# A double first group, w in two halves of columns, and tiles that hold every fourth column

## The chip, the cores and the metric

The kernel runs on one core of a Trainium2 chip. The metric is the time of one execution on the device in microseconds (us). "Fast" is the undisturbed state. A time is about 2 us longer than the span that the profile of the same execution shows; times are compared with times, spans with spans. TensorE is written PE in the profile (PEld is its weight load), VectorE is DVE, ScalarE is ACT, GpSimd is POOL, SyncE is SP.

## The reference

```python
B, S, D = (16, 2048, 1024)          # x: [B, S, D], w: [D, D], decay: [D], all float32
xw = x @ w
out[:, 0, :] = xw[:, 0, :]
for t in range(1, S):
    out[:, t, :] = decay[None, :] * out[:, t - 1, :] + xw[:, t, :]
```

A matrix product, then along time a running sum that decays with its own factor in each of the 1024 columns.

## The kernel before

Time is cut into 64 chunks of 512 steps. Chunks go in double groups of 1024 steps, but the first two and the last two chunks are groups of their own. A "tile" is 128 columns of the product for one group, with the columns on the partitions and time along the row, along which the kernel scans. A chunk of x is loaded as bf16 (GpSimd issues it), turned in blocks of 32x32 by VectorE (`turn`), and copied into order by VectorE or ScalarE (`part`). Eight matmuls for each chunk and tile make the product. In three of four tiles ScalarE and GpSimd first fold pairs of steps (`pair`), VectorE scans half the elements, and the other half is filled in (`complete`); every fourth tile is scanned whole by VectorE straight from PSUM. Then VectorE turns the result back into row order (`back`), and it is stored.

The parts that the change touches:

```python
    def matmul(ps, n, k, xt, t0=0, t1=TL):          # n: tile, k: step of the contraction
        pin(nc.tensor.matmul(
            out=ps[:, t0:t1],
            lhsT=wsb[:, k, n].rearrange("p q i -> p (q i)"),      # 128 columns, packed
            rhs=xt[:, k // 2, k % 2, t0:t1],
            start=(k == 0), stop=(k == K - 1)))
    # ... (cut)
        def back(self):
            T, n = self.T, self.n
            pin(nc.vector.transpose(
                out=self.ot[:, :, n * P:(n + 1) * P],             # 32 floats in a row, packed
                in_=self.so[:, 2:T + 2].rearrange("p (i t) -> p i t", t=P)))
            if n == 3:
                self.store(0, 4)
            elif n == 5 and self.final:
                self.store(4, 6)
            elif n == 7:
                self.store(6 if self.final else 4, 8)

        def store(self, n0, n1):
            for q in (0, 2, 1, 3):
                queue = nc.scalar if self.final and q >= 2 else nc.sync
    # ... (cut): the DMA of quarter q
    # head: w comes as whole rows in bf16, and eight copies bring it into the order that wsb has
    for k in range(K):
        copy = nc.scalar.copy if k % 4 == 3 else nc.vector.tensor_copy
        pin(copy(out=wsb[:, k].rearrange("p n q i -> p q n i"), in_=wk[:, k]))
    # ... (cut)
    # single-chunk groups: two tiles share one PSUM tile
                    if n % 2 == 0:
                        both = ring(psp, "ps", 3, [128, 2, TL])
                    ps = both[:, n % 2]
```

Of the kernel before, what the change touches and what calls it, by code (L numbers as in the profile page):

```python
# [9 lines left out]
FP32 = mybir.dt.float32  # L10
BF16 = mybir.dt.bfloat16
ALU = mybir.AluOpType


def _ap(ap_obj: bass.AP, new_ap, extra_offset=0):
    return dataclasses.replace(
        ap_obj,
        ap=[list(p) for p in new_ap],
        offset=ap_obj.offset + extra_offset,
    )  # L20
# [5 lines left out]
def kernel(  # L26
# [21 lines left out]



    nc = tc.nc
    pin = tc.keep_in_program_order
    B, S, D = x.shape
    assert w.shape == (D, D)

    NQ = 4
    P = 32
    CQ = D // NQ
    K = CQ // P
# [1 line left out]
    TL = 512  # L61
    NJ = TL // P
    NC = S // TL
    HEADS = 7

    const = ctx.enter_context(tc.tile_pool(name="const", bufs=1))
    sb = ctx.enter_context(tc.tile_pool(name="sb", bufs=1))
# [8 lines left out]
    def quad(q):  # L76
        return slice(q * P, (q + 1) * P)

    chunks = [(b, c * TL) for b in range(B) for c in range(NC)]
    nch = len(chunks)  # L80
    groups = ([[0], [1]] + [[c, c + 1] for c in range(2, nch - 2, 2)]
              + [[nch - 2], [nch - 1]])
    for g in groups:
        assert chunks[g[0]][0] == chunks[g[-1]][0]

    dec = const.tile([128, K], FP32, name="dec")
    dec2 = psp.tile([128, 512], FP32, name="dec2")
    spare = psp.tile([128, TL], FP32, name="spare")
    wsb = const.tile([128, K, K, NQ, P], BF16, name="wsb")

    def ot_tile():
        return ring(sb, "ot", 2, [128, 2 * NJ, CQ])
# [29 lines left out]
    def matmul(ps, n, k, xt, t0=0, t1=TL):  # L122
        pin(nc.tensor.matmul(  # L123
            out=ps[:, t0:t1],
            lhsT=wsb[:, k, n].rearrange("p q i -> p (q i)"),
            rhs=xt[:, k // 2, k % 2, t0:t1],
            start=(k == 0),
            stop=(k == K - 1),
        ))
# [3 lines left out]
    class Tile:  # L133
# [42 lines left out]
        def scan(self):  # L176
            T, n, so = self.T, self.n, self.so
            if self.paired:
                pin(nc.vector.tensor_tensor_scan(  # L179
                    out=so[:, 3:T + 2:2],  # L180
                    data0=dec2[:, n:n + 1].to_broadcast([128, T // 2]),
                    data1=self.xs[:, 1:T:2],
                    initial=0.0 if self.prev is None else self.prev,
                    op0=ALU.mult,
                    op1=ALU.add,
                ))
            else:
                pin(nc.vector.tensor_tensor_scan(  # L188
                    out=so[:, 2:T + 2],
                    data0=dec[:, n:n + 1].to_broadcast([128, T]),  # L190
                    data1=self.ps,
                    initial=0.0 if self.prev is None else self.prev,
                    op0=ALU.mult,
                    op1=ALU.add,
                ))

        def complete(self):
            T, so = self.T, self.so
# [7 lines left out]
        def back(self):  # L206
            T, n = self.T, self.n
            pin(nc.vector.transpose(  # L208
                out=self.ot[:, :, n * P:(n + 1) * P],
                in_=self.so[:, 2:T + 2].rearrange("p (i t) -> p i t", t=P)))  # L210
            if n == 3:
                self.store(0, 4)
            elif n == 5 and self.final:
                self.store(4, 6)
            elif n == 7:
                self.store(6 if self.final else 4, 8)

        def store(self, n0, n1):
            for q in (0, 2, 1, 3):
                queue = nc.scalar if self.final and q >= 2 else nc.sync  # L220
                pin(queue.dma_start(
                    out=_ap(out, [[D, P], [P * D, self.T // P], [1, (n1 - n0) * P]],
                            (self.b * S + self.t0) * D + q * CQ + n0 * P),
                    in_=self.ot[quad(q), :, n0 * P:n1 * P]))


    with nc.allow_non_contiguous_dma(reason="a vector of 1024"):
        for q in range(NQ):
            nc.sync.dma_start(
                out=dec[quad(q), :], in_=_ap(decay, [[1, P], [P, K]], q * CQ))  # L230
    idle = const.tile([128, TL], BF16, name="idle")
    pin(nc.vector.memset(idle, 0.0))  # L232
    for _ in range(40):
        pin(nc.tensor.matmul(out=spare, lhsT=idle[:, 0:128], rhs=idle, start=True, stop=True))  # L234
    H = NJ // 2
    for j0 in (0, H):
        for q in range(NQ):
            load(0, q, j0, j0 + H)
    wb = ot_tile().rearrange("p j c -> p (j c)")[:, 0:M * D].bitcast(BF16)
    wm = wb.rearrange("p (m d) -> p m d", m=M)  # L240
    for m in range(M):
        for q in range(NQ):
            pin(nc.gpsimd.dma_start(  # L243
                out=wm[quad(q), m],
                in_=_ap(w, [[2 * D, P], [1, 2 * D]], (q * CQ + m * 2 * P) * D)))
    for j0 in (0, H):
        for q in range(NQ):
            load(1, q, j0, j0 + H)
    for q in range(NQ):
        load(2, q)  # L250
    for j0 in (0, H):
        turn(0, j0, j0 + H)
        part(0, nc.vector.tensor_copy, 0, 2, j0, j0 + H)
        part(0, nc.scalar.copy, 2, M, j0, j0 + H)
    pin(nc.vector.tensor_tensor(out=dec2[:, 0:K], in0=dec, in1=dec, op=ALU.mult))
    wk = wb.rearrange("p (k q n i) -> p k q n i", k=K, q=NQ, n=K)
    for k in range(K):
        copy = nc.scalar.copy if k % 4 == 3 else nc.vector.tensor_copy
        pin(copy(out=wsb[:, k].rearrange("p n q i -> p q n i"), in_=wk[:, k]))  # L259


    agenda = {}
# [2 lines left out]
    def at(step, f, *args):  # L265
        agenda.setdefault(step, []).append(lambda: f(*args))

    def turn_and_load(c):
        turn(c)
        if c + 3 < nch:  # L270
            loads.extend((c + 3, q) for q in range(NQ))

    def turn_last_half(c):
        turn(c, H, NJ)
        loads.extend((c + 3, q) for q in range(NQ))

    at(1, turn, 1, 0, H)
    at(1, part, 1, nc.vector.tensor_copy, 0, 2, 0, H)
    at(1, part, 1, nc.scalar.copy, 2, M, 0, H)
    at(3, turn_last_half, 1)  # L280
    at(3, part, 1, nc.vector.tensor_copy, 0, 2, H, NJ)
    at(3, part, 1, nc.scalar.copy, 2, M, H, NJ)
    for gi, g in enumerate(groups):
        for l, c in enumerate(g):
            if c > 1:
                first = gi * K
                ahead = (7, 6, 4) if l or len(g) == 1 else (11, 10, 8)
                at(first - ahead[0], turn_and_load, c)
                at(first - ahead[1], part, c, nc.scalar.copy, 0, 2)
                at(first - ahead[2], part, c, nc.scalar.copy, 2, M)  # L290

    waiting = []

# [16 lines left out]
            if tl is not None and tl.paired == lag:  # L310
                tl.back()

    loads.extend((3, q) for q in range(NQ))
    for gi, g in enumerate(groups):
        T = TL * len(g)
        if len(g) == 2:
            ot = ot_tile()
        else:
            if g[0] in (0, nch - 2):
                halves = ot_tile()  # L320
            ot = halves[:, g[0] % 2 * NJ:(g[0] % 2 + 1) * NJ]
        heads = []
        if gi == 0:
            bank = [ring(psp, "ps", 3, [128, 2, TL]) for _ in range(3)]
            heads = [bank[n // 2][:, n % 2] for n in range(6)] + [spare]
            for k in range(K):
                for n in range(HEADS):
                    matmul(heads[n], n, k, xt_of[0])
        elif gi == 1:
            bank = [ring(psp, "ps", 3, [128, 2, TL]) for _ in range(2)]  # L330
            heads = [bank[n // 2][:, n % 2] for n in range(4)]
            for t0 in (0, H * P):
                for n in range(4):
                    for k in range(K):
                        matmul(heads[n], n, k, xt_of[1], t0, t0 + H * P)
        for n in range(K):
            if n < len(heads):
                ps = heads[n]
            else:
                if len(g) == 2:  # L340
                    ps = ring(psp, "ps", 3, [128, T])
                elif gi == 0:
                    ps = ring(psp, "ps", 3, [128, 2, TL])[:, 0]
                else:
                    if n % 2 == 0:
                        both = ring(psp, "ps", 3, [128, 2, TL])
                    ps = both[:, n % 2]
                for k in range(K):
                    for l, c in enumerate(g):
                        matmul(ps[:, l * TL:(l + 1) * TL], n, k, xt_of[c])  # L350
            behind(Tile(gi, n, ps, ot))
            for f in agenda.pop(gi * K + n, []):
                f()
            for _ in range(2 if len(loads) > NQ else 1):
                if loads:
                    load(*loads.pop(0))
    behind(None)
    behind(None)


# [1 line left out]
_INS = ['x', 'w', 'decay']  # L362
_OUTS = [((16, 2048, 1024), 'float32')]
# [25 lines left out]
```

## Time and profile before

| what | before |
|---|---|
| time, median of 3 runs | 953.86 us (953.14 to 954.48) |
| matmuls | 4096 of 512 columns' worth, 0.2155 us each in the middle |
| TensorE busy, VectorE busy | 95%, 87% of the span |
| first 144 matmuls done | 69.6 us |
| from there to the start of the last two chunks | 825.3 us |
| from there to the end of the last back-transpose | 42.0 us |
| from there to the end of the span | 16.6 us |

The last four rows cut the span of 953.6 us at marks that I count out of the matmul rows of the trace: the moment at which 144 matmuls are done, and the moment at which 3968 are (all but the 128 of the last two chunks). The lines of the profile that show the bound stand in the prediction.

### The profile page before, as it was taken

What the parts mean: (1) busy time and instruction counts of PE and PEld (TensorE: products, weight loads), DVE (VectorE), ACT (ScalarE), POOL (GpSimd) and SP (SyncE); (2) the same over time, 40 slices, a digit from 0 to 9 for tenths busy, and PEclk for the clock granted to TensorE, in tenths of its full rate; (3) what the DMA queues carried; (4) which work ended last, traced back from release to release, by engine and by line L of the source; (5) the groups of instructions that cost most, each with busy time, mean ns of one, the idle gap of its engine ahead of it and who ended that gap; (6) DMA issues with size and microseconds to landing.
All of it is one profiled execution on the core that took longest, in us unless ns stands there. A gap on an engine that the chain in (4) does not pass through costs nothing. (4 is left out here: it accounts for less than half of the span.)

```text
span 953.6 us, 12026 instructions
## 1 busy us (share of the span) xinstructions
PE 904.8 (95%) x4168; PEld 410.6 (43%) x4168; DVE 830.6 (87%) x622; ACT 684.9 (72%) x961; POOL 663.1 (70%) x768
## 2 busy tenths in 40 slices
PE   8669999999999999999999999999999999999871
PEld 3334444444444444444444444444444444444330
DVE  2678999999999999999999999999999999998872
ACT  2468777877777787778777777877787787776550
POOL 8557777777776777777677777767776776765430
PEclk9789999999999999999999999999999999999997
DMA  9999999999999999999999999999999999996628
GB/s 161 170 218 172 223 234 232 225 224 235 224 227 228 237 227 223 233 227 229 226 235 225 228 228 229 231 221 233 224 236 225 229 229 224 234 229 148 145 49 188
DMA packets 405821, 204.23 MB, mean 214 GB/s; under 512 B 14080, under 2 KB 405248, under 8 KB 405760
## 3 DMA queue, kind: packets, MB, share of 16 engines
q1 hardware_dynamic: 266528, 133.19, 57.5%
q0 software_dynamic: 136064, 69.22, 54.0%
q10 hardware_dynamic: 3168, 1.05, 0.6%
q8 instruction: 32, 0.52, 0.2%
q14 instruction: 29, 0.24, 0.1%
HBM read 138.42 MB, written 134.22 MB: 286 GB/s over the span
## 5 line engine op out<-in xcount | busy, mean ns | idle before, releaser
L123 PE MATMUL ps<-xt,wsb 128*128 128x512 bf16 (+1 forms) x4120 | 893.8, 380 | 28.4 <-ACT h L157 16.7
L123 PEld LDWEIGHTS <-wsb 128*128 128x128 bf16 x4128 | 406.4, 98 | 516.6 <-issue 36.0
L173 POOL TENSOR_TENSOR xs<-h,xs 128x512 f32<-128x512 f32 (+1 forms) x195 | 244.7, 1255 | 212.3 <-ACT h L157 92.6
L167 ACT COPY xs<-ps 128x1024 f32<-128x1024 f32 (+1 forms) x194 | 190.4, 982 | 186.1 <-PE ps L123 183.1
L208 DVE STREAM_TRANSPOSE ot<-so 128x1024 f32<-128x1024 f32 (+1 forms) x272 | 303.5, 1154 | 2.2 <-POOL so L201 1.3
L201 POOL TENSOR_TENSOR so<-h,xs 128x512 f32<-128x512 f32 (+1 forms) x195 | 243.6, 1249 | 44.7 <-ACT keep L204 22.4
L120 ACT COPY xt<-xw 128x2048 bf16<-128x2048 bf16 (+1 forms) x128 | 240.1, 1876 | 17.6 <-DVE xw L112 17.6
L102 POOL DMA_DIRECT2D xb<-in_x_dram x264 | 174.8, 663 | 7.9 <-DVE xw L112 6.0
L157 ACT ACTIVATE h<-so,dec 128x512 f32<-128x512 f32 (+1 forms) x195 | 147.3, 755 | 33.4 <-DVE so L179 29.7
L179 DVE TENSOR_TENSOR_SCAN so<-dec,keep,xs 128x512 f32<-128x512 f32 (+1 forms) x101 | 123.6, 1224 | 42.8 <-POOL xs L173 42.5
L112 DVE STREAM_TRANSPOSE xw<-xb 128x2048 f32<-128x2048 f32 (+1 forms) x66 | 146.6, 2221 | 8.1 <-DMA xb<-in_x_dram 8.1
L179 DVE TENSOR_TENSOR_SCAN so<-dec,xs 128x512 f32<-128x512 f32 (+1 forms) x94 | 113.0, 1202 | 41.5 <-POOL xs L173 38.1
L157 ACT ACTIVATE h<-ps,dec 128x512 f32<-128x512 f32 (+1 forms) x194 | 131.5, 678 | 0.0
L188 DVE TENSOR_TENSOR_SCAN so<-dec,keep,ps 128x1024 f32<-128x1024 f32 (+1 forms) x43 | 86.2, 2004 | 4.8 <-PE ps L123 4.6
L188 DVE TENSOR_TENSOR_SCAN so<-dec,ps 128x1024 f32<-128x1024 f32 (+1 forms) x34 | 72.6, 2135 | 0.0
L204 ACT COPY keep<-so 128x1 f32<-128x1 f32 x144 | 26.9, 187 | 0.2 <-DVE so L188 0.2
L172 ACT COPY so<-keep 128x1 f32<-128x1 f32 x101 | 19.3, 191 | 0.0
L234 PE MATMUL spare<-idle 128*128 128x512 bf16 x40 | 10.3, 424 | 1.2 <-DVE idle L232 1.2
L170 POOL MEMSET so<- 128x1 f32 x94 | 11.0, 117 | 0.0
L243 POOL DMA_DIRECT2D ot<-in_w_dram x16 | 8.4, 529 | 2.4 <-DMA xb<-in_x_dram 1.2
L259 DVE COPY wsb<-ot 128x1024 bf16<-128x1024 bf16 x6 | 2.4, 424 | 6.1 <-DMA ot<-in_w_dram 6.1
L234 PEld LDWEIGHTS <-idle 128*128 128x128 bf16 x40 | 4.2, 108 | 6.8 <-issue 1.9
(12 smaller groups left out, 11.3 us busy)
## 6 DMA issues: line engine op xcount, KB each, us to landing
out_dram<-ot SPq DMA_DIRECT2D x240, 512.0 KB, 9.0
xb<-in_x_dram POOLq DMA_DIRECT2D x248, 256.0 KB, 7.5
out_dram<-ot SPq DMA_DIRECT2D x26, 256.0 KB, 6.5
xb<-in_x_dram POOLq DMA_DIRECT2D x16, 128.0 KB, 5.1
ot<-in_w_dram POOLq DMA_DIRECT2D x16, 128.0 KB, 4.8
out_dram<-ot ACTq DMA_DIRECT2D x2, 256.0 KB, 3.5
out_dram<-ot ACTq DMA_DIRECT2D x4, 128.0 KB, 4.0
out_dram<-ot SPq DMA_DIRECT2D x4, 128.0 KB, 3.5
```

What stands on the lines that cost most here:

```text
L102: pin(nc.gpsimd.dma_start(out=xb_of[c][quad(q), j0:j1], in_=_ap(x, [[D, P], [P * D, j1 - j0], [1, CQ]], (b * S + t0 + j0 * P) * D + q * CQ)))
L112: pin(nc.vector.transpose(out=dst.rearrange("p (m j i) -> p j m i", m=M, i=P)[:, j0:j1], in_=src.rearrange("p (j m c) -> p j m c", m=M, c=P)))
L120: pin(copy(out=xt_of[c][:, m0:m1, :, j0 * P:j1 * P], in_=src))
L123: pin(nc.tensor.matmul(out=ps[:, t0:t1], lhsT=wsb[:, k, n].rearrange("p q i -> p (q i)"), rhs=xt[:, k // 2, k % 2, t0:t1], start=(k == 0), ...
L157: pin(nc.scalar.activation(out=h, in_=src, func=mybir.ActivationFunctionType.Copy, scale=dec[:, self.n:self.n + 1]))
L167: pin(nc.scalar.copy(out=self.xs, in_=self.ps))
L173: pin(nc.gpsimd.tensor_tensor(out=self.xs[:, 1:T:2], in0=g, in1=self.xs[:, 1:T:2], op=ALU.add))
L179: pin(nc.vector.tensor_tensor_scan(out=so[:, 3:T + 2:2], data0=dec2[:, n:n + 1].to_broadcast([128, T // 2]), data1=self.xs[:, 1:T:2], init ...
L188: pin(nc.vector.tensor_tensor_scan(out=so[:, 2:T + 2], data0=dec[:, n:n + 1].to_broadcast([128, T]), data1=self.ps, initial=0.0 if self.pr ...
L201: pin(nc.gpsimd.tensor_tensor(out=so[:, 2:T + 2:2], in0=h, in1=self.xs[:, 0:T:2], op=ALU.add))
L204: pin(nc.scalar.copy(out=self.keep, in_=so[:, T + 1:T + 2]))
L208: pin(nc.vector.transpose(out=self.ot[:, :, n * P:(n + 1) * P], in_=self.so[:, 2:T + 2].rearrange("p (i t) -> p i t", t=P)))
```

## The change

Its intent is to shorten both ends. Chunks 0 and 1 become a double group. w comes in two halves of columns, so that matmuls can start on the lower half. The copies that reorder w go: w stays as it is in memory, a tile takes every fourth column of a half, and the price is a stride of four in the weight load and in what the back-transpose writes. At the end each tile gets its own PSUM tile, chunk 63 is turned earlier, and all stores go on one queue.

```diff
-    groups = ([[0], [1]] + [[c, c + 1] for c in range(2, nch - 2, 2)]
-              + [[nch - 2], [nch - 1]])
+    groups = [[c, c + 1] for c in range(0, nch - 2, 2)] + [[nch - 2], [nch - 1]]
-    wsb = const.tile([128, K, K, NQ, P], BF16, name="wsb")
+    wsb = const.tile([128, K, D], BF16, name="wsb")
-            lhsT=wsb[:, k, n].rearrange("p q i -> p (q i)"),
+            lhsT=wsb[:, k, n // R * CH + n % R:(n // R + 1) * CH:R],     # R = 4, CH = 512
...
-                out=self.ot[:, :, n * P:(n + 1) * P],
+                out=self.ot[:, :, n // R * CR + n % R:(n // R + 1) * CR:R],     # CR = 128
-            if n == 3: ...
+            if n % R == R - 1:
+                self.store(n // R)
...
-                queue = nc.scalar if self.final and q >= 2 else nc.sync
+                pin(nc.sync.dma_start(
...
+    def lower(m):      # SyncE, fp32 to a stage; cast(m): DVE and ACT write it to wsb[:, k, 0:CH]
+    def upper(m):
+        for q in range(NQ):
+            pin(nc.gpsimd.dma_start(
+                out=wsb[quad(q), 2 * m:2 * m + 2, CH:D],
+                in_=_ap(w, [[2 * D, P], [D, 2], [1, CH]], (q * CQ + m * 2 * P) * D + CH)))
...
-    for q in range(NQ):
-        load(2, q)
...
+    steps = {2: (3, 3, 4), 3: (4, 5, 6), 4: (7, 8, 10), nch - 1: (-11, -10, -8)}
...
-    loads.extend((3, q) for q in range(NQ))
+    loads.extend((c, q) for c in (2, 3, 4) for q in range(NQ))
...
-                        both = ring(psp, "ps", 3, [128, 2, TL])
-                    ps = both[:, n % 2]
+                if len(g) == 2 or n % 4 < 3:
                     ps = ring(psp, "ps", 3, [128, T])
+                else:
+                    ps = ring(psp, "spare", 1, [128, TL])
```

Cut: the order of the first loads, the order of the first matmuls, and the scan of a tile that lies in two PSUM tiles.

## The prediction

Cut from it, where marked, is what it said of the hardware that no run or trace of this case shows: most of one paragraph, one ground for rival 1 and half a sentence of rival 3. The sum came to 926.5 us, taken as 925. Three of its figures need their source, and all three are in the trace of the kernel before. The 1.04 ns an element of a transpose is (2285 - 1217) / 1024, from the mean times for 2048 and 1024 elements. These 1068 ns for 1024 more elements are also the 1067 of rival 1; that the new step would cost as much again ("at half rate") was my assumption. The 2 ns of a scan is (2260 - 1192) / 512, from whole-row scans of 1024 and 512 elements. Half clock is the granted clock of 0.50 from 14.5 to 17.9 us, where matmuls of 512 columns start 0.43 us apart.

> **What bounds the kernel now.** I read the page first, then the busy time of each engine in stretches, then the waits of TensorE, the start and end in order of time, and last the waits of SyncE's queue.
>
> ```profile
> PE 904.8 (95%) x4168; PEld 410.6 (43%) x4168; DVE 830.6 (87%) x622; ACT 684.9 (72%) x961; POOL 663.1 (70%) x768
> ...
> PEclk9789999999999999999999999999999999999997
> ```
> ```profile
> 100.00:300.00 200.00, 200.00 (x928) 90.68 (x927) 184.99 (x131) 156.22 (x214) 148.78 (x169) 1.00 1.19 228
> ```
> The last line has busy us of PE, PEld, DVE, ACT and POOL, each with its count, then clock, DMA share and GB/s. From 100 to 880 us every such stretch is full of matmuls: 200 us by 928 is 0.2155 us each. The middle is TensorE's; DVE is next with 92.5%, so about 15 us of every 200 are free. The work is 64 chunks by 8 column tiles by 8 steps of k = 4096 matmuls; by 0.2155 that is 882.7 us. So 953.6 - 882.7 = 71 us lie at the two ends, and only they can be won.
>
> ```profile
> PE ps L123 <- ACT h L157: 16.7, 9, 6.6
> PE ps L123 <- DVE so L188: 9.0, 4, 2.9
> PE ps L123 <- DVE wsb L259: 2.7, 1, 2.7
> ```
> ```profile
> 14.20 2.50 PE L123 MATMUL ps<-xt,wsb 128*128 128x512 bf16 x6 [2.71 <-DVE wsb L259]
> ...
> 57.37 6.02 PE L123 MATMUL ps<-xt,wsb 128*128 128x512 bf16 x16 [6.59 <-ACT h L157]
> ...
> 64.44 10.74 PE L123 MATMUL ps<-xt,wsb 128*128 128x512 bf16 x49 [1.05 <-ACT h L157]
> ```
> The head: the first useful matmul is at 14.20, and TensorE is continuous only from 64.44. By my count of the rows 120 matmuls are done by then (25.9 us of work in 50.2 us): idle 15.3 us before it, and half clock around 14.5 to 17.9, 31.6 to 45.2 and 55.4 to 62.3 in the clock record. The single-chunk groups 0 and 1 pay a start-up of the chain copy, add, scan for only 8 matmuls a tile.
>
> ```profile
> 908.94 3.61 PE L123 MATMUL ps<-xt,wsb 128*128 128x512 bf16 x16 [1.58 <-ACT h L157]
> ...
> 927.44 0.92 ACTq L221 DMA_DIRECT2D out_dram<-ot  x2
> ...
> 935.70 1.28 DVE L208 STREAM_TRANSPOSE ot<-so 128x512 f32<-128x512 f32 x2
> ```
> ```profile
> SPq L221 <- DMA out_dram<-ot: 31.6, 4, 25.8
> ```
> ```profile
> 910.00:920.00 10.00, 7.90 (x37) 3.42 (x36) 7.28 (x10) 4.40 (x14) 2.94 (x4) 1.00 0.02 6
> ```
> The tail has two faults. Each pair of tiles shares one two-bank PSUM tile, and the second half waits until ACT has read the first: one wait per 16 matmuls, 10.4 us in all from 897.90. And SyncE's stores stand still for 25.8 us: the DMA share is 0.02 from 910 to 920 although chunk 62 has finished halves. The semaphore that its first store waits for is the one of a store that ACT's queue issued at 927.44 and that landed at 930.44. Eighteen stores then go out after 930; the last back-transpose ends at 936.98, the span at 953.6: 16.6 us of draining.
>
> [...] The trace has only packed loads, 98 ns each. [...] Four bf16 are 8 bytes[...]. But the new back-transpose writes fp32 with a step of four, 16 bytes[...]. No instruction of this trace writes so, and this is the largest open point.
>
> **The change, part by part.**
> (a) Head. Chunks 0 and 1 become a double group; w comes in two column halves, the lower by SyncE as fp32 and cast on chip, the upper cast in the DMA straight to its place. Tiles 0 to 3 need only the lower half, and with the stride a tile holds every fourth column of a half; the loads of the upper half queue behind chunk 1. The copies that reordered w on chip go (eight, 0.42 us on DVE and 1.04 on ACT); eight casts of 512 columns take their place, inside the wait for chunk 0. In the issue rows of the head, transfers of 256 KB read landed 0.63 to 0.70 us apart, about 0.4 MB per us. The last load of chunk 0 landed at 11.07. The first quarter of lower w adds 0.5 MB (1.2 us, part of it in an idle queue), and the rest shares the engines with the end of chunk 0, say 1.5 us: landing near 13.5. Transpose 1.25 and copy 0.69 give a first matmul near 15.5, 1.3 later than now. Thirty-two matmuls, eight at half clock (0.43 each, as at 14.2 now): 24.1. Chunk 1 is in by then (6.3 MB at 0.416 from about 4.5 is 19.6; with its transpose and copy 22). Thirty-two half matmuls of 0.11 to 27.6, 16 full ones to 31.0. Tile 4 ends at 34.4, tile 5 at 37.9. Now the chain behind TensorE must keep up, with these durations of one instruction (busy us in all, then mean ns, after the bar):
>
> ```profile
> L208 DVE STREAM_TRANSPOSE ot<-so 128x1024 f32<-128x1024 f32 x240 | 282.9, 1217 | 0.8
> L120 ACT COPY xt<-xw 128x2048 bf16<-128x2048 bf16 x124 | 235.9, 1903 | 5.0 <-DVE xw L112 5.0
> L173 POOL TENSOR_TENSOR xs<-h,xs 128x512 f32<-128x512 f32 x180 | 233.6, 1298 | 198.6 <-ACT h L157 89.3 <-ACT so L172 58.0 <-issue 45.8
> L167 ACT COPY xs<-ps 128x1024 f32<-128x1024 f32 x180 | 182.3, 1013 | 171.9 <-PE ps L123 168.9 <-POOL so L201 1.4 <-issue 0.2
> L157 ACT ACTIVATE h<-ps,dec 128x512 f32<-128x512 f32 x180 | 124.8, 693 | 0.0
> ```
> Tile 0 is complete at 26.7; copy 1.01 and scale 0.69 bring it to 28.4, POOL's add 1.30 to 29.7. Chunk 2 is loaded only behind that add, because POOL works in program order: two issues of 0.66 to 31.0, tile 1's add to 32.3, tile 0's second add to 33.6, two issues to 34.9. The last part lands near 39.5, 4.6 after its issue, as the first quarter-chunk loads did (3.9 to 5.2). DVE is then at 41.0 with the scans of tiles 2 and 3 and tile 1's transpose, so chunk 2 is turned at 43.3 and its first copy on ACT ends at 45.2. That copy stands ahead of tile 4's eviction in ACT's order, which ends at 46.9. TensorE meanwhile: tile 6 waits for tile 3's scan until 39.9 and ends at 43.3, tile 7 waits for tile 4's bank until 46.9. Chunk 3 lands near 46, is turned at 48.3 and copied by 57.6, after the evictions of tiles 4 to 6. The first tile of chunks 2 and 3 is so complete at 57.6 + 8 x 0.2155 = 59.3, and with some half clock after two long waits at 60.5. That is 144 matmuls. Before, the same 144 were done at 64.44 + 24 x 0.2155 = 69.6. Gain: 9.1 us.
> (b) Steady part. The same counts of every instruction; the weight load has 215 - 98 = 117 ns of room, the back-transpose about 0.26 us (15 us by some 58 transposes in 200 us). Zero, if both strides are free.
> (c) Tail, arithmetic. Each tile has its own PSUM tile, four in turn, so the wait on the other half goes; chunk 63's transpose (2.29) and copies move into the double group before. TensorE would need 128 x 0.2155 = 27.6 us for the last two chunks. DVE has 6.35 us of older work when they start (895.15 to 901.5 now), then per two tiles a paired scan 0.63, a scan 1.19 and two transposes 1.20, 3.02 for eight pairs, and 0.6 for the unpaired tile 6: 31.1. With 1.4 for latencies DVE ends 32.5 after that start; now 936.98 - 895.15 = 41.8. Gain: 9.3 us.
> (d) Tail, stores. All go on one queue in order, so chunk 62 leaves while chunk 63 is computed. The last four stores of 256 KB follow the last transpose. Four issued at 901.54 landed 2.3 us apart for 512 KB, the first after 4.5: 2.1 + 4 x 1.15 = 6.7 us, and 0.9 as now from the last landing to the end: 7.6 in place of 16.6. Gain: 9.0 us.
> Sum: 953.9 - 9.1 - 9.3 - 9.0 = 926.5; I take 925, as chunk 2's landing was read on the late side.
>
> **The rivals.**
> 1. The 16-byte step makes the back-transpose slow. At half rate, 1024 elements cost 1217 + 1067 ns = 2.28 us, and 240 of them 256 us more: DVE passes 1090 us busy and sets the pace, about 1130 in all. Below 0.26 us extra it stays hidden. For it: [...]the 92.5% of DVE. Against: the scans that write with a step of 8 bytes cost 1.23 us for 512 elements, no more for each than the packed ones (2.26 us for 1024); but a scan takes some 2 ns an element and the transpose 1.04, so it proves little. Also against, the weaker kind of evidence: DVE is so near its limit that a change with this cost would hardly have been worked out to such detail. I give it one in seven.
> 2. Strided weight loads become slow. Twice 98 ns is still under 215 and hidden. Only beyond that would each nanosecond cost 4.1 us; I give 3%.
> 3. The head gives nothing: lower w and chunk 0 collide, or chunk 2 comes later still[...]. For it: the order of POOL's queue. Then 934 to 940.
> 4. The head is better than I read it: chunk 2 lands at 37 and tile 7 does not wait. Then 915 to 919.
> 5. The last stores still drain slowly because one queue issues all: SyncE's issues took up to 1.8 us each at the end. Then 3 us more.
>
> **Range and chances.** With free strides, my three gains have errors of some 6, 3 and 3 us: 911 to 945 holds nearly all of that. Faster by over 2% (under 934.8) 0.74; within 2% 0.10, mostly rival 3; slower 0.16, rivals 1 and 2. The range leaves the slow case out.
>
> **What would show it.** The mean of the 1024-element back-transpose stays near 1217 ns and PEld near 98 ns (rivals 1 and 2 if not); the middle stretches keep 928 matmuls in 200 us; TensorE's waits on ACT's h in the last 60 us are gone; SyncE's wait on a store's DMA no longer has a 25.8 us case, and the DMA is busy through the last chunk; from the last transpose to the end it is 7 to 8 us; 144 matmuls are done by 58 to 62 us. I am wrong if DVE is the engine without idle time in the middle, or if TensorE waits longer in the first 70 us than now.

## The result, and the profile after

The changed kernel takes 1047.14 us (median of 4 runs, 1046.66 to 1048.39), the kernel before in the same rounds 954.17 us. The ratio is 1.0976, with a 95% interval of 1.0957 to 1.0995: slower by 9.8%. A ratio here is the mean time of one kernel's fast runs over the mean time of the other's of the same rounds, so it is not quite the ratio of the medians.

First the page of the changed kernel: the busy times, and the row of VectorE in 40 slices of the span.

```profile
PE 918.2 (88%) x4152; PEld 473.0 (45%) x4152; DVE 997.9 (95%) x605; ACT 681.6 (65%) x945; POOL 671.6 (64%) x767
...
DVE  3479999999999999999999999999999999999996
```

TensorE and VectorE have changed places: 88% and 95%, where it was 95% and 87%. One stretch of the middle, with the columns as in the prediction:

```profile
100.00:300.00 200.00, 182.37 (x837) 94.90 (x836) 200.00 (x118) 138.72 (x186) 135.71 (x152) 1.00 1.15 213
```

VectorE is busy for all of the 200 us, and 837 matmuls are done in place of 928. The groups by shape (busy us in all and mean ns of one after the first bar) name the operation:

```profile
L216 DVE STREAM_TRANSPOSE ot<-so 128x1024 f32<-128x1024 f32 x248 | 496.2, 2084 | 1.2 <-POOL so L209 1.1
L125 PEld LDWEIGHTS <-wsb 128*128 128x128 bf16 x4112 | 468.7, 114 | 549.2 <-issue 137.6 <-ACT xt L122 7.6 <-DVE wsb L247 0.6
```

The back-transpose takes 2084 ns where it took 1217, and the weight load 114 ns where it took 98. And TensorE waits (us in all, times, longest):

```profile
PE ps L125 <- DVE so L195: 92.1, 62, 4.2
PE ps L125 <- DMA wsb<-in_w_dram: 6.7, 1, 6.7
```

Line 195 is the whole-row scan, with which VectorE releases a PSUM tile: it comes late once in each half group, 62 times. In order of time, TensorE's rows near 510 us (start, duration, count, idle before):

```profile
506.73 13.97 PE L125 MATMUL ps<-xt,wsb 128*128 128x512 bf16 x64 [1.34 <-DVE so L195]
522.28 10.09 PE L125 MATMUL ps<-xt,wsb 128*128 128x512 bf16 x46 [1.57 <-DVE so L195]
```

And VectorE at the same place, three back-transposes in a row, first of the kernel before, then of the changed one:

```profile
511.26 3.47 DVE L208 STREAM_TRANSPOSE ot<-so 128x1024 f32<-128x1024 f32 x3
```
```profile
506.61 5.92 DVE L216 STREAM_TRANSPOSE ot<-so 128x1024 f32<-128x1024 f32 x3
...
522.16 5.90 DVE L216 STREAM_TRANSPOSE ot<-so 128x1024 f32<-128x1024 f32 x3
```

A half group is four tiles, 64 matmuls. VectorE's period for it is 522.16 - 506.61 = 15.55 us (15.44 on average from 200 to 880 us), TensorE's work 64 x 0.2155 = 13.79. From the beginning of one instruction to that of the next, VectorE needs on average (300 to 860 us) 1.92 us for a back-transpose, 1.12 for a paired scan, 2.21 for a whole scan and 2.20 for the transpose of a chunk: 4 x 1.92 + 3 x 1.12 + 2.21 + 2.20 = 15.45. So the period is VectorE's work, with nothing else in it. In the kernel before VectorE was busy for 184.99 of 200 us, that is 12.75 of each 13.79: 1.04 us were free, and with the longer transposes VectorE needs 15.44 - 12.75 = 2.7 us more.

The head has a wait that nobody had foreseen. After the first four matmuls TensorE stops for 6.7 us for a DMA of w:

```profile
15.25 1.44 PE L125 MATMUL ps<-xt,wsb 128*128 128x512 bf16 x3 [3.65 <-DVE xt L122]
...
23.86 1.44 PE L125 MATMUL ps<-xt,wsb 128*128 128x512 bf16 x3 [6.74 <-DMA wsb<-in_w_dram]
```

Those matmuls need the lower half alone, which comes through the stage and the casts; the tile that a DMA writes directly is the upper half. SyncE's long wait for a store, 25.8 us before, is gone. What is left of its waits for stores stands at the very end:

```profile
SPq L404 <- DMA out_dram<-ot: 2.8, 3, 1.1
```

Where the span went, in us. The predicted column holds the marks of its steps (a), (c) and (d), and for (b), "zero", the middle of before. The last three columns are experiments told below: `back_packed`, `before_strided` and `regroup_later`.

| part | before | predicted | after | back_packed | before_strided | regroup_later |
|---|---|---|---|---|---|---|
| to 144 matmuls done | 69.6 | 60.5 | 68.9 | 67.9 | 70.0 | 57.9 |
| to the start of the last two chunks | 825.3 | 825.3 | 922.5 | 832.5 | 909.7 | 827.3 |
| to the end of the last back-transpose | 42.0 | 32.5 | 46.1 | 33.6 | 51.2 | 33.5 |
| to the end of the span | 16.6 | 7.6 | 7.4 | 7.5 | 16.4 | 5.8 |
| span | 953.6 | 925.9 | 1045.0 | 941.5 | 1047.3 | 924.5 |

After the change the span is 119.1 us longer than predicted: 8.4 in the head, 97.2 in the middle, 13.6 in the tail, -0.2 in the drain. A column is one profiled execution. In `back_packed` that was the slowest of four (943.56 us, median 939.59), so its parts together are some 4 us longer than in a usual run; in `before_strided` it was the slowest too (1049.09, median 1047.32).

### The profile page after: what moved, and what is told of

It reads as the page before. It is cut to its first block, busy times and chain, and to the rows that moved or that the text cites. A ratio compares the mean times of both kernels' runs of the same rounds, so it can differ in the third digit from the quotient of the medians.

```text
span 1045.0 us, 11949 instructions
## 1 busy us (share of the span) xinstructions
PE 918.2 (88%) x4152; PEld 473.0 (45%) x4152; DVE 997.9 (95%) x605; ACT 681.6 (65%) x945; POOL 671.6 (64%) x767
## 5 line engine op out<-in xcount | busy, mean ns | idle before, releaser
L125 PE MATMUL ps<-xt,wsb 128*128 128x512 bf16 x4072 | 899.2, 381 | 108.9 <-DVE so L195 92.1
L125 PEld LDWEIGHTS <-wsb 128*128 128x128 bf16 x4112 | 468.7, 114 | 549.2 <-issue 137.6
L216 DVE STREAM_TRANSPOSE ot<-so 128x1024 f32<-128x1024 f32 (+1 forms) x264 | 512.5, 2025 | 3.1 <-POOL so L209 3.0
L175 POOL TENSOR_TENSOR xs<-h,xs 128x512 f32<-128x512 f32 (+1 forms) x193 | 249.6, 1293 | 88.4 <-ACT h L159 43.6
L169 ACT COPY xs<-ps 128x1024 f32<-128x1024 f32 (+1 forms) x193 | 191.6, 993 | 11.7 <-PE ps L125 11.7
L181 DVE TENSOR_TENSOR_SCAN so<-dec,xs 128x512 f32<-128x512 f32 x96 | 113.7, 1184 | 17.0 <-POOL xs L175 17.0
L181 DVE TENSOR_TENSOR_SCAN so<-dec,keep,xs 128x512 f32<-128x512 f32 (+1 forms) x97 | 116.1, 1198 | 0.0
L195 DVE TENSOR_TENSOR_SCAN so<-dec,keep,ps 128x1024 f32<-128x1024 f32 (+1 forms) x35 | 75.6, 2163 | 0.0
L195 DVE TENSOR_TENSOR_SCAN so<-dec,ps 128x1024 f32<-128x1024 f32 x31 | 70.3, 2266 | 0.0
L125 PE MATMUL spare<-xt,wsb 128*128 128x512 bf16 x40 | 12.0, 416 | 1.3 <-DVE so L195 1.3
L241 POOL DMA_DIRECT2D wsb<-in_w_dram x16 | 8.7, 551 | 5.1 <-DMA xb<-in_x_dram 4.9
L253 PE MATMUL spare<-idle 128*128 128x512 bf16 x40 | 10.4, 427 | 1.2 <-DVE idle L251 1.2
```

What stands on the lines that cost most here:

```text
L125: pin(nc.tensor.matmul(out=ps[:, t0:t1], lhsT=wsb[:, k, n // R * CH + n % R:(n // R + 1) * CH:R], rhs=xt[:, k // 2, k % 2, t0:t1], start=( ...
L169: pin(nc.scalar.copy(out=self.xs, in_=self.ps))
L175: pin(nc.gpsimd.tensor_tensor(out=self.xs[:, 1:T:2], in0=g, in1=self.xs[:, 1:T:2], op=ALU.add))
L181: pin(nc.vector.tensor_tensor_scan(out=so[:, 3:T + 2:2], data0=dec2[:, n:n + 1].to_broadcast([128, T // 2]), data1=self.xs[:, 1:T:2], init ...
L195: pin(nc.vector.tensor_tensor_scan(out=so[:, t:t + size], data0=dec[:, n:n + 1].to_broadcast([128, size]), data1=ps, initial=before, op0=A ...
L216: pin(nc.vector.transpose(out=self.ot[:, :, n // R * CR + n % R:(n // R + 1) * CR:R], in_=self.so[:, 2:T + 2].rearrange("p (i t) -> p i t" ...
```

## The experiments

Theory: the back-transpose that writes every fourth float (a step of 16 bytes) is the loss, and nothing else in the change costs much. Rivals: the strided weight load; the new order of head and tail; the large spread of what a transpose writes, whatever its step.

### 1 to 3. Which of the two strides

Each is the changed kernel with one line altered. The columns then come out in a wrong order, so all three give a wrong result; sizes and counts of all work stay.

`back_packed`, the back-transpose packed as before:

```diff
-                out=self.ot[:, :, n // R * CR + n % R:(n // R + 1) * CR:R],
+                out=self.ot[:, :, n * P:(n + 1) * P],
```

> The changed kernel with one line undone: the back-transpose writes each tile's 32 columns side by side, as before, and the weights are still read with a step of four. The columns of the result come out in a wrong order on purpose. Theory A (the 16-byte step of the back-transpose's output is the whole loss): a 1024-element back-transpose takes about 1.22 us again, VectorE has idle time in the middle, 928 matmuls in 200 us, and the time is what is left of the head, tail and store gains: 953.9 - 0.4 - 9.3 - 9.0, about 935 us. Theory B (the strided weight loads, 98 to 114 ns, hold TensorE back as well): fewer than 928 matmuls in 200 us and over 945 us. Theory C (the new order of work, not the step, fills VectorE): transposes short again but the time stays over 1000 us.

`weights_packed`, the weight load packed:

```diff
-            lhsT=wsb[:, k, n // R * CH + n % R:(n // R + 1) * CH:R],
+            lhsT=wsb[:, k, n * 128:(n + 1) * 128],
```

> The changed kernel with the other stride undone: each weight load reads 128 columns side by side, and the back-transpose still writes with a step of four (wrong result on purpose). Theory A: PEld goes back to 98 ns and nothing else changes, 1040 to 1050 us, about 830 matmuls in 200 us. Theory B: most of the loss goes, under 1000 us.

`back_step2`, the back-transpose with a step of two floats, 8 bytes:

```diff
-                out=self.ot[:, :, n // R * CR + n % R:(n // R + 1) * CR:R],
+                out=self.ot[:, :, n // 2 * 64 + n % 2:(n // 2 + 1) * 64:2],
```

> The changed kernel with the back-transpose's output at a step of two fp32, 8 bytes, in place of four (two tiles share 64 columns; wrong order of columns on purpose). [...]the transpose is at its packed time of 1.22 us or little above, and the time is near the run with the packed output, about 935 us. If any step other than one costs, it stays near 2.1 us and the time near 1047.

| run | time, us | ratio to before (95%) |
|---|---|---|
| back_packed | 939.59 (938.41 to 943.56) | 0.9854 (0.9829 to 0.9879) |
| back_step2 | 939.68 (938.54 to 939.76) | 0.9844 (0.9827 to 0.9860) |
| weights_packed | 1036.11 (one look; the state of a single run is not known) | |

The group of the back-transpose and a stretch of the middle in `back_packed`:

```profile
L216 DVE STREAM_TRANSPOSE ot<-so 128x1024 f32<-128x1024 f32 x248 | 292.5, 1217 | 9.8 <-DMA out_dram<-ot 7.2 <-POOL xs L175 1.7
```
```profile
300.00:500.00 200.00, 200.00 (x928) 105.32 (x927) 184.53 (x131) 156.29 (x210) 149.49 (x166) 1.00 1.19 229
```

The same group in `back_step2`:

```profile
L216 DVE STREAM_TRANSPOSE ot<-so 128x1024 f32<-128x1024 f32 x248 | 293.1, 1222 | 6.4 <-DMA out_dram<-ot 5.4
```

And the two groups in `weights_packed`:

```profile
L216 DVE STREAM_TRANSPOSE ot<-so 128x1024 f32<-128x1024 f32 x248 | 493.4, 2083 | 1.1 <-POOL so L209 1.1
L125 PEld LDWEIGHTS <-wsb 128*128 128x128 bf16 x4112 | 404.1, 98 | 602.8 <-issue 134.3 <-DVE wsb L247 0.6
```

With the transposes packed and everything else of the change kept, 1217 ns and 928 matmuls are back, and 107.6 us with them. The strided weight load stays in that kernel and costs nothing in its middle. A step of 8 bytes is as good as none (1222 ns), so it is not striding as such: the cost comes between 8 and 16 bytes. With the weights packed instead, the transposes stay at 2083 ns, and only 11 us come back (the time is below the 1040 to 1050 that I had expected): 7.8 of them in the head, where the wait on the DMA of w disappears and 144 matmuls are done at 61.1 us. `back_packed` came 4.6 us above the 935 that I had expected; its head is no shorter than that of the whole change, and its middle is longer than before.

### 4. The steps by themselves

A separate small kernel: runs of ten equal instructions on one operand, only the step altered; 40 matmuls for each step of the weights. Its output is incomplete.

```python
    def spread(s):      # 1024 floats, s floats apart
        return dst[:, 0:1024 * s].rearrange("p (i t s) -> p i t s", t=P, s=s)[:, :, :, 0]
    for _ in range(10):
        pin(nc.vector.transpose(out=spread(4), in_=blocks))     # likewise 1, 2, 3, 6, 8
    # ... the same with nc.scalar.copy, on its output and on its input (steps 1, 2, 4, 8)
    for _ in range(40):
        pin(nc.tensor.matmul(out=ps[2], lhsT=wb[:, 0:128 * 4:4], rhs=rhs, start=True, stop=True))
```

> A kernel that does nothing but the disputed instructions, ten of each in a row with no other engine on the same data: back-transposes of 1024 fp32 with output steps of 1, 2, 3, 4, 6 and 8; copies on ScalarE with output steps and with input steps of 1, 2, 4 and 8 fp32; weight loads of 128 bf16 columns with steps of 1, 2, 4, 8, 16 and 32. [...]transposes with steps 1 and 2 at about 1.2 us, 3 in between, 4, 6 and 8 all near 2.1 us. If it is contention in the full kernel and not the step, step 4 is at 1.2 us here. Weight loads: 98 ns for 1, about 114 for 4, and[...] a jump at 8 and above[...]; whether it then passes the 215 ns of a matmul is open. The result is wrong on purpose.

The groups: VectorE packed and with steps of 2, 3, 4 and 8 floats (lines 59, 61, 63, 65, 69), ScalarE's output with 2 and 4 (lines 73 and 75), the weight load with steps of 2 and 8 bf16 (lines 89 and 93):

```profile
L65 DVE STREAM_TRANSPOSE dst<-src 128x1024 f32<-128x1024 f32 x10 | 20.4, 2041 | 0.3
...
L69 DVE STREAM_TRANSPOSE dst<-src 128x1024 f32<-128x1024 f32 x10 | 20.2, 2018 | 0.3
L75 ACT COPY dst<-src 128x1024 f32<-128x1024 f32 x10 | 19.9, 1988 | 0.3
...
L63 DVE STREAM_TRANSPOSE dst<-src 128x1024 f32<-128x1024 f32 x10 | 16.1, 1612 | 0.3
L61 DVE STREAM_TRANSPOSE dst<-src 128x1024 f32<-128x1024 f32 x10 | 12.5, 1246 | 0.3
L59 DVE STREAM_TRANSPOSE dst<-src 128x1024 f32<-128x1024 f32 x10 | 12.4, 1239 | 0.3
...
L73 ACT COPY dst<-src 128x1024 f32<-128x1024 f32 x10 | 11.0, 1105 | 0.3
...
L93 PEld LDWEIGHTS <-wb 128*128 128x128 bf16 x40 | 5.7, 143 | 2.9
...
...
L89 PEld LDWEIGHTS <-wb 128*128 128x128 bf16 x40 | 3.9, 98 | 4.7
```

Packed, the transpose takes 1239 ns. It is free up to 8 bytes (1246), costs 30% at 12 (1612) and 65% at 16 (2041), and no more beyond (1964 at 24 bytes, 2018 at 32). So the cost is one of the step, not of the distance that is covered. ScalarE's copy behaves much alike, though 8 bytes are not quite free for it (1044 packed, 1105 or 6% more, 1988), and reading with a step costs it the same as writing (1108 and 1988). For each element the 16 bytes cost VectorE 0.8 ns more ((2041 - 1239) / 1024) and ScalarE 0.9 ((1988 - 1044) / 1024). The weight load rises from 98 to 113 ns at 8 bytes and to 143 at 16, where it stays (145 and 144 at 32 and 64); in each of the five strided groups the 40 matmuls took 8.80 us, so none of it is seen under a matmul of 512 columns. (The packed group came first, its 40 matmuls took 11.57 us, with weight loads 0.43 us apart up to 17 us, and it is no measure.) The changed kernel's 114 ns and 2084 ns agree with the 113 and 2041 here.

### 5. Keep the plan, give up the strides: `regroup`

If the theory holds, the plan can be had without its cost. Here a tile still belongs to one half of the columns, but its columns are four blocks of 32 that lie packed; the casts, which run anyway, write w into that order, and eight small copies of VectorE do so for the upper half. The result is correct.

```diff
-    wsb = const.tile([128, K, D], BF16, name="wsb")
+    wsb = const.tile([128, K, K, NQ, P], BF16, name="wsb")
-            pin(copy(out=wsb[:, 2 * m + e, 0:CH], in_=stage[:, m, e]))
+            regroup(copy, 2 * m + e, 0, stage[:, m, e])
+    def regroup(copy, k, h, src):
+        pin(copy(out=wsb[:, k, h * R:(h + 1) * R].rearrange("p r q i -> p q r i"),
+                 in_=src.rearrange("p (q r i) -> p q r i", q=NQ, r=R)))
+    for k in range(K):      # after chunk 1 is turned
+        regroup(nc.vector.tensor_copy, k, 1, wup[:, k // 2, k % 2])
```

(and `matmul` and `back` packed as before, the upper half loaded beside the stage, decay in the order of the tiles.)

> A correct kernel with the changed kernel's groups, loads, tail and stores, but with the weights put back in blocks of 32 columns by the casts (lower half) and by eight VectorE copies out of a staging area (upper half), so that the back-transpose writes side by side and weight loads are packed. No DMA writes the weights themselves. If the two losses found are the step of the back-transpose and TensorE's wait for the upper half's DMA after the fourth matmul, both are gone: 144 matmuls done near 61 us (61.1 in the run with packed weights), tail 33.6, drain 7.5, so 61 + 826 to 832 + 33.6 + 7.5 = 928 to 934 us. If the wait for the upper half's data were real need and not a tracking of overlaps, the 144th comes near 68 and the time is near 939.

Measured: 935.99 us (935.26 to 936.50), ratio 0.9809 (0.9794 to 0.9823): 2 us above the 928 to 934 that I had expected. The same plan is 1.9% faster than the kernel before once the back-transposes are packed. But `before_tail` below, with the old head, takes 935.92 us: all of this gain can be had from the tail alone, and the new head pays only in runs 10 to 12.

### 6. Is the wait on the upper half of w the head's loss: `packed_rows`

`back_packed`, with each row of the upper half in its own DMA (wrong order of columns, as there):

```diff
-            pin(nc.gpsimd.dma_start(
-                out=wsb[quad(q), 2 * m:2 * m + 2, CH:D], ...
+            for e in range(2):
+                pin(nc.gpsimd.dma_start(
+                    out=wsb[quad(q), 2 * m + e, CH:D], ...
```

> The run with the packed back-transpose (939.6 us; weights still strided; wrong order of columns on purpose), with each DMA of the upper half of w cut in two so that it writes one row of 512 columns and not two rows with a lower half between them. If TensorE's wait of 7 us for the upper half's DMA after four matmuls is there because the two-row write spans the lower half that the strided load reads, the wait goes, 144 matmuls are done near 61 us in place of 67.9, and the time is 932 to 934 us. If it waits for the DMA for another reason, the first 70 us stay as they are, or get longer by the 16 more issues of about 0.5 us on the DMA queue of GpSimd.

Measured: 938.79 us (938.40 to 943.82), ratio 0.9854: no gain over `back_packed`, where I had expected one. The wait after the fourth matmul is gone: the 32 matmuls of chunk 0 are done by 23.9 us in place of some 32. But TensorE then stands at other places, first for the same DMA (0.40 us at 33.09, and 2.78 at 37.01), and then for ScalarE:

```profile
37.01 1.06 PE L125 MATMUL ps<-xt,wsb 128*128 128x512 bf16 x4 [2.78 <-DMA wsb<-in_w_dram]
```

TensorE's last restart of the head on a copy of x came at 64.16 us, at 64.98 in `back_packed`. One thing follows: the wait of 6.7 us was no need of the data. It is there where a strided slice of the weights is read and one DMA writes the halves of two rows, and gone where either is altered (`weights_packed`, this run). That the program's bookkeeping takes the two for overlapping is my inference; no row of the trace says it.

It does not follow that the wait is without weight for the head, because this run put another delay in its place, the one that the end of its expectation names. GpSimd issues 32 DMAs for the upper half in place of 16, and its first addition, behind which chunk 2 is loaded, comes after them. First its rows in this run, then the first addition in `weights_packed`:

```profile
22.52 13.21 POOL L242 DMA_DIRECT2D wsb<-in_w_dram  x26 [0.19 <-issue]
...
35.87 1.29 POOL L175 TENSOR_TENSOR xs<-h,xs 128x512 f32<-128x512 f32 x1
```
```profile
30.38 1.28 POOL L175 TENSOR_TENSOR xs<-h,xs 128x512 f32<-128x512 f32 x1 [2.00 <-ACT h L159]
```

In `back_packed` the same addition starts at 36.50, after GpSimd has waited 8.02 us for ScalarE, which waits for the matmuls. So chunk 2 is asked for at 37.74 us in `back_packed`, at 37.10 here and at 31.62 in `weights_packed`, where the wait goes without more issues; there 144 matmuls are done at 61.1 us in place of 67.9. As far as that single look shows, the wait costs the head some 7 us, by way of chunk 2.

### 7 and 8. The tail alone, in the kernel before

`before_one_queue` is the kernel before with all stores on SyncE; `before_tail` adds a PSUM tile for each tile of the last two chunks, the earlier turn of chunk 63, and the last half stored whole. Both are correct.

```diff
-                queue = nc.scalar if self.final and q >= 2 else nc.sync
+                queue = nc.sync
```
```diff
+                if c == nch - 1:
+                    ahead = (11, 10, 8)
+                elif gi > 1:
+                    ps = ring(psp, "ps" if n % 4 < 3 else "spare", 3 if n % 4 < 3 else 1, [128, TL])
```

> The kernel before with one edit: the last chunk's stores all go on SyncE's queue. By the prediction's part (d) SyncE no longer stands for 25.8 us, the drain from the last back-transpose to the end falls from 16.6 to about 7.5 us and the time by 9, to 944.5 us. The rival: one queue has to issue the same 24 stores after 901, so the drain stays above 12 us and the time above 949.

> The kernel before with the whole tail of the change and nothing else: stores in one queue, each tile of the last two chunks in its own PSUM tile, chunk 63 transposed and copied earlier, the last half stored whole. A correct kernel. From the start of the last two chunks to the last back-transpose 33.6 us in place of 42.0 and a drain of 7.5 in place of 16.6: 953.7 - 8.4 - 9.1 = 936 us. If the tail's gain needs the new head or the strided layout, it stays above 942.

Measured: 942.12 us (941.65 to 944.46), ratio 0.9879 (0.9864 to 0.9893); and 935.92 us (935.53 to 936.24), ratio 0.9808 (0.9794 to 0.9823); the kernel before in these rounds 953.80. The one queue alone is worth 11.7 us: the drain falls from 16.6 to 4.9. In `before_one_queue` SyncE no longer waits for any store but the last:

```profile
SPq L384 <- DMA out_dram<-ot: 1.5, 3, 0.6
```

That is better than the 7.4 of the changed kernel. One difference is that the kernel before stores its last half in two pieces, while a stride of four across the half makes it complete only when all four tiles are done; `regroup_pieces` below finds 1.2 us for that, so it is at most part of the cause. In `before_tail` the drain is 7.4, and from the last back-transpose of 1024 elements to the last of all it takes 27.0 us in place of 35.5: 8.5 + 9.2 = 17.7 us of gain, against 9.3 + 9.0 in the prediction. Tail and drain of the change are worth what was predicted, and need neither stride.

### 9. The stride alone, in the kernel before: `before_strided`

```diff
-                out=self.ot[:, :, n * P:(n + 1) * P],
+                out=self.ot[:, :, n // 4 * 128 + n % 4:(n // 4 + 1) * 128:4],
```

(with the last half stored whole; wrong order of columns.)

> One part of the change alone, put into the kernel before: its back-transposes write every fourth element (16 bytes apart); packed weights, old head, old tail, old stores stay (the last half is stored whole, as pieces of it are no longer complete; the columns are in a wrong order on purpose). Theory that the 16-byte step of the back-transpose is the whole loss: mean near 2.08 us, VectorE without idle time in the middle, about 830 matmuls in 200 us, 62 half groups of 1.76 us more, and slower single-chunk groups at both ends: 1055 to 1070 us, ratio about 1.11. Rival, that the loss needs the strided weight loads or the new order of the head beside it: under 1000 us.

Measured: 1047.32 us (1045.41 to 1049.09), ratio 1.0969 (1.0944 to 1.0994). Under the expected 1055 to 1070, far from the rival's under 1000. The middle and the back-transposes:

```profile
300.00:500.00 200.00, 182.28 (x836) 81.64 (x835) 200.00 (x119) 139.43 (x192) 135.35 (x152) 1.00 1.11 206
```
```profile
L208 DVE STREAM_TRANSPOSE ot<-so 128x1024 f32<-128x1024 f32 x240 | 474.9, 2063 | 2.2 <-POOL so L170 1.1 <-POOL so L201 1.1
```

One line makes the kernel before as slow as the whole change did. That is also the most telling number: with packed transposes the rest of the change is worth 14 us (953.65 to 939.59), with strided ones nothing (1047.32 to 1047.14). When VectorE sets the pace, the time is VectorE's work, plus its idle time, plus the drain. Both kernels have 997 us of work (997.2 and 997.9). Up to its last transpose VectorE is idle for 1030.9 - 997.2 = 33.7 us in `before_strided` and 1037.6 - 997.9 = 39.7 in the changed kernel: in the first 80 us it did 53.57 and 43.31 us of work, since the new head feeds it later. The 9.0 us that the drain gains (16.4 to 7.4) are mostly given back there, 6.0 of them. In the profiled spans 2.3 us are left, in the medians nothing.

### 10 to 12. What still binds the head

`regroup_early` is `regroup` with chunk 2 loaded right after the upper half of w, before GpSimd's first addition, and chunks 2 and 3 turned earlier. `regroup_pieces` is that with the last half stored in two pieces. `regroup_later` is that with chunk 2 turned one step later again. All are correct.

```diff
+    for q in range(NQ):
+        load(2, q)                          # after upper(m)
-    steps = {2: (3, 3, 4), 3: (4, 5, 6), ...
+    steps = {2: (1, 1, 2), 3: (3, 4, 5), ...        # regroup_later: 2: (2, 2, 3)
-    loads.extend((c, q) for c in (2, 3, 4) for q in range(NQ))
+    loads.extend((c, q) for c in (3, 4) for q in range(NQ))
```
```diff
+            if n == 3: self.store(0, 4)             # regroup_pieces, regroup_later
+            elif n == 5 and self.final: self.store(4, 6)
+            elif n == 7: self.store(6 if self.final else 4, 8)
```

> The run with the regrouped weights, with chunk 2 loaded before the first addition of GpSimd, turned two steps earlier, and chunk 3 turned one step earlier. Theory that the head sets the time from chunk 2's path: the head's last restart on a copy of x comes at about 58 in place of 62.1, and the time falls from 936.0 to about 932. Rival, that VectorE, with 7.5% of room only, and the queue of stores have the backlog to work off whatever the head wins: the middle gets longer by what the head gains, and the time stays within 1.5 us of 936.

> The run before in this call, with the last half of the last chunk stored in two pieces, as soon as two of its four tiles are done; possible only because the tiles lie packed. The drain should fall from 7.4 to about 4.9 us, as in the run with one queue in the kernel before: 2.5 us less than the run before in this call, 929 to 931 if that one gives 932. If the earlier stores delay the last transposes or the last store waits longer for its turn, no gain.

> The last run with chunk 2 still loaded early, but turned after tile 2's second addition instead of tile 1's, one step later in the order of VectorE and ScalarE. In the run before, chunk 2 landed at 39.7 and its transpose stood in VectorE's order 4.0 us before it could run; ScalarE's evictions of tile 2 stood behind it, and TensorE had one wait of 9.4 to 10.5 us for their h. Theory that this place in the order is what costs: the wait falls under 5 us, and the time from 931.6 to 928 or 929. Rival, that VectorE's backlog takes it back: the waits come up elsewhere in the first 180 us and the time stays at 931 to 933.

| run | time, us | ratio to before (95%) | 144 matmuls done | drain |
|---|---|---|---|---|
| regroup_early | 932.58 (932.48 to 934.07) | 0.9773 (0.9755 to 0.9791) | 61.5 | 7.2 |
| regroup_pieces | 931.61 (931.11 to 932.24) | 0.9758 (0.9744 to 0.9773) | 63.3 | 6.0 |
| regroup_later | 926.54 (926.29 to 926.70) | 0.9711 (0.9698 to 0.9725) | 57.9 | 5.8 |

The time of `regroup_early` came as expected, but not by the restart that I had named: there was none of that kind any more. Instead chunk 2 was asked for too soon. VectorE, ScalarE and TensorE in order of time:

```profile
39.71 2.31 DVE L114 STREAM_TRANSPOSE xw<-xb 128x2048 f32<-128x2048 f32 x1 [4.02 <-DMA xb<-in_x_dram]
```
```profile
42.05 1.90 ACT L122 COPY xt<-xw 128x2048 bf16<-128x2048 bf16 x1 [5.50 <-DVE xw L114]
```
```profile
45.50 19.63 PE L125 MATMUL ps<-xt,wsb 128*128 128x512 bf16 x80 [9.39 <-ACT h L159]
```

VectorE stood 4.0 us for chunk 2, ScalarE stood behind it with the evictions of a tile whose PSUM TensorE needed, and TensorE stood 9.4 us. The pieces saved 1.2 us in the drain (7.2 to 6.0), not the 2.5 expected, and the medians differ by 1.0 us; why the drain stays above the 4.9 of `before_one_queue` stays open. With the transpose one step later, TensorE's waits in `regroup_later` are:

```profile
PE ps L125 <- DVE so L195: 4.0, 2, 2.4
...
PE ps L125 <- ACT h L159: 2.0, 1, 2.0
```

The 10.5 us of `regroup_pieces` (9.4 in `regroup_early`) have become 2.0, and 5.1 us came off the time (931.61 to 926.54), more than I had expected; it did not come back in the middle (827.3 us, 827.7 in `regroup_pieces`). This kernel beats both: 27.3 us, or 2.9%, faster than the one before.

## Why the prediction was wrong, by its own steps

- **(b) failed**: "Zero, if both strides are free". The condition was half true. The weight load rose from 98 to 114 ns under 215 and was hidden, as reckoned (rival 2 falls). The back-transpose was not free, and its room of "about 0.26 us" was right: 1.04 us for each four. They needed 2.7. The excess, 15.44 - 13.79 = 1.65 us, for some 60 half groups (3824 matmuls of the middle by 64) makes 99 us; the middle grew by 97.2 over the prediction.
- **Rival 1 was the truth and had too small a chance.** The prediction gave it one in seven. Its two grounds against it were weak: a scan takes 2.09 ns an element and a transpose 1.04, so the one proves little for the other, as the prediction itself says, and its step of 8 bytes costs a transpose next to nothing either (1246 against 1239 ns); and that "a change with this cost would hardly have been worked out" tells nothing of the chip. Of its two grounds for it one held: with the only instruction in doubt on an engine 92.5% busy, even odds would have been fair.
- **Its size was off**: "about 1130", measured 1047. The term is the cost of one transpose, taken as 1.067 us more, the assumed half rate. The row shows 0.87 more (2084 - 1217), and on the path it counts less still, 2.7 / 4 = 0.68: with VectorE never idle, each instruction starts a little before the last one's end (three transposes in a row take 5.92 us, not 6.25). With four times 1.067 less 1.04, the middle would have grown by 60 x 3.2 = 194 us.
- **(a) failed too, by 7 to 8 us**: 144 matmuls at 68.9 (67.9 with packed transposes), not 60.5. The step that failed is "Thirty-two matmuls, eight at half clock (0.43 each, as at 14.2 now): 24.1": TensorE stood 6.7 us after the first four, which the working had not, and the 32 were done at 32.1. Tile 0's addition on GpSimd, put at 28.4 to 29.7, began at 36.6, and chunk 2 was asked for behind it at 37.9. The rest of the chain was read well. In `weights_packed`, without that wait, chunk 2's transpose starts at 43.6 and ends 45.9 (predicted 41.0 and 43.3), the last copy of chunk 3 ends at 59.6 (57.6), and 144 matmuls are done at 61.1. With chunk 2 loaded early and turned at the right step it is 57.9.
- **(c) and (d) were right** where VectorE has room: 33.6 against 32.5, and 7.5 against 7.6 (`back_packed`); `before_tail` shows them alone. In the changed kernel (c) is 46.1, because the work there is VectorE's as well.
- **Not in the sum at all**: the middle after a late head is longer than before, by 7.2 us in `back_packed` (its profile is the slowest of its four runs) and by 4.1 in `back_step2`. VectorE has little room there, and once it waits for a store (7.2 and 5.4 us); that it is working off a backlog of the head is my reading, and no run isolates it. The time of `back_packed` lies where rival 3 puts it (934 to 940).
- **Small slips in its readings.** The four stores that landed about 2.3 us apart are those issued at 887.73; at 901.54 only three went out, 2.5 to 2.6 us apart. Of the 10.4 us of waits from 897.90, 1.4 were for a scan of VectorE. Rival 1's 240 transposes make 830.6 + 256 = 1087 us, not over 1090. And the half clock in the first 70 us began at 14.5, 31.6 and 55.4 us, after TensorE had been idle for 2.71, 2.62 and 4.67 us (in the first two cases it had started again 0.3 and 0.8 us earlier); what sets it off is not shown.

Its signs to look for were well chosen: the mean of the back-transpose and "VectorE is the engine without idle time in the middle" gave the answer at the first look.

## What to carry to other kernels

Reckon a stride in bytes, on the operand that a nearly full engine reads or writes, and time that one instruction by itself before counting it free: here, on VectorE's transpose, 8 bytes were free and 16 cost 65% (1246 and 2041 ns, packed 1239). The room of the second-busiest engine is a number (1.04 us in each 13.79), and once the cost had passed it (2.7 us), the gains made elsewhere no longer counted (14 us with packed transposes, none with strided ones). The early load paid in full only when what waits for it stood late enough in the order of each engine: one step moved TensorE's wait from 10.5 us to 2.0, and the time from 931.61 to 926.54 us. And a run that takes one delay away must be looked through for the one that it brings (`packed_rows`).
